# Casts ahead of transposes in the front of a batched product, and 14 small loads behind its last store

## The chip, the cores and the metric

The kernel runs on one core of one Trainium2 chip. The metric is device time in microseconds (us). The kernel before took 306.07 us, the median of three runs (305.9 to 306.18). A core has five engines that run side by side and meet only at semaphores: PE (TensorE, matrix products), DVE (VectorE), ACT (ScalarE), POOL (GpSimd) and SP (SyncE, which here only issues DMAs). Sixteen DMA engines move data between memory and the on-chip buffers.

## The reference

```python
batch, n_heads, seq_t, seq_s, channels = 8, 12, 512, 512, 64

def reference(x, y):
    return np.einsum('bhtc,bhsc->bhts', x, y).astype(np.float32)
```

There are 96 independent products of a 512x64 matrix with the transpose of another 512x64 matrix. Inputs and outputs are float32. The inputs are 25.17 MB in all and the output is 100.66 MB.

## The kernel before

**Tiling.** The 96 heads form six groups of 16. One group of x, or of y, is a contiguous block of 2 MB: 128 partitions of 64 rows with 64 channels each. So there are 12 loads; load 2g is x of group g, load 2g+1 is y of group g. A group has two halves, and half i (0 to 11, `NH` of them) gives two output tiles t = 2i and 2i+1. There are 24 tiles t; each is 128 partitions by 8192 float32 (4 MB) and is written by one store.

**Buffers.** Three large slots (`slot`, 4 MB each) serve as landing place of the loads and later as staging of the output tiles. A load takes half a slot (`place` 0 to 5), a store a whole one. Since the slots are shared, a load or an output tile can only enter where what was there has been read. `xk` keeps x of a group in bf16 and `yb` keeps y of half a group in bf16. `xb`, of which there is only one, holds x of one half rearranged for the transpose. `xT` and `yT` hold the transposed operands, two of each, one for even and one for odd halves.

**Steps.**
- `load(n, place)` (DMA issue on SP, L126) fetches a group.
- `keep_x(n)` (ACT, L114) casts 128x4096 x to bf16 in `xk`.
- `keep_y(n, half)` casts the 64 partitions of a half in two instructions, one for each half of the channels, on the engines that `in_front` names: DVE and POOL for half 0, DVE and ACT for half 1 (L116 for DVE and POOL, L114 for ACT).
- `mix(i, engine, parts)` copies x of half i from `xk` to `xb` in four parts of 32 partitions (L116).
- `turn_x(i)` and `turn_y(i)` are transposes on DVE (L184 and L197).
- `quarter(t, s, k, "act")` is eight matmuls into `pm` in PSUM (L212) and an eviction of 128x2048 from `pm` to a quarter of the slot on ACT (L114).
- `store(t, s)` (DMA issue on SP, L233) writes the slot to memory.

**Order.** Every engine runs its instructions in the order in which the code emits them; `emit` works out from what each reads and writes which semaphores it has to wait for (L82 where a wait stands alone). SP is such an engine too: if the next load waits for a cast, every later load and store stands behind it. A load into a half slot waits for the casts that read it (a y load for ACT, POOL and DVE). All loads and stores go through one DMA queue.

The front (from L238 to `store(2, 1)`) is written out by hand, with six loads issued at once and six more as half slots come free. Its part around the change, in the order before:

```python
        load(7, 3)
        mix(1, "pool", range(1, 4))
        turn_x(1)
        keep_x(4)
        load(8, 4)
        quarter(0, 0, 0, "act")
        keep_y(5, 0)
        keep_y(5, 1)
        load(9, 5)
        turn_y(1)
```

Behind the front a loop over t = 3 to 23 makes four quarters and a store for each tile, and prepares half i+2 on DVE after each odd t. At the end SP waits for the last store of each of the three slots.

Of the kernel before, what the change touches and what calls it, by code (L numbers as in the profile page):

```python
# [9 lines left out]
def kernel(  # L10
# [22 lines left out]
    nc = tc.nc  # L33
# [14 lines left out]
    fp32 = mybir.dt.float32  # L48
# [5 lines left out]
    xv = x.rearrange("b h t c -> (b h t c)").rearrange("(g p n) -> g p n", p=P, n=R * C)  # L54
# [5 lines left out]
    sb = ctx.enter_context(tc.tile_pool(name="sb", bufs=1))  # L60
# [2 lines left out]
    xks = [sb.tile([P, R, C], bf16, name=f"xk{i}") for i in range(NG - 1)]  # L63
    ybs = [sb.tile([P, R // 2 * D], u32, name=f"yb{i}") for i in range(2 * NG - 3)]
    xb = sb.tile([P, K * E * D], u32, name="xb")
    xTs = [sb.tile([P, K * D * E], u32, name=f"xT{i}") for i in range(2)]
    yTs = [sb.tile([P, D * R // 2], u32, name=f"yT{i}") for i in range(2)]
    pms = [ps.tile([P, 4, S], fp32, name=f"pm{i}") for i in range(2)]
    engines = {"act": nc.scalar, "dve": nc.vector, "pool": nc.gpsimd, "pe": nc.tensor, "sp": nc.sync}
    sems, ticks, known, snaps, writer, readers = {}, {}, {e: {} for e in engines}, {}, {}, {}  # L70

    def need(name, points):

        best = {}
        for p, v in points:
            if known[name].get(p, 0) < v:
                best[p] = max(best.get(p, 0), v)
        for p, v in list(best.items()):
            if any(snaps[q, w].get(p, 0) >= v for q, w in best.items() if q != p):
                del best[p]  # L80
        for p, v in best.items():
            engines[name].wait_ge(sems[p], v)  # L82
            known[name][p] = v
            for q, w in snaps[p, v].items():
                known[name][q] = max(known[name].get(q, 0), w)

    def emit(name, make, reads=(), writes=(), dma=None):

        points = [writer[r] for r in (*reads, *writes) if r in writer]
        points += [v for w in writes for v in readers.get(w, ())]  # L90
        if name == "pool" and name in ticks:
            points.append((name, ticks[name]))
        need(name, points)
        p, step = (name, 1) if dma is None else (f"dma{dma}", 16)
        if p not in sems:
            sems[p] = tc.alloc_semaphore(p)
        make().then_inc(sems[p], step)
        at = (p, ticks.get(p, 0) + step)
        ticks[p] = at[1]
        snaps[at] = {**known[name], p: at[1]}  # L100
        if dma is None:
            snaps[at][name] = at[1]
        for r in reads:
            readers.setdefault(r, []).append(at)
        for w in writes:
            writer[w], readers[w] = at, []
# [4 lines left out]
    def copy(name, dst, src, reads, writes):  # L111
        emit(
            name,
            lambda: nc.scalar.activation(dst, src, COPY)  # L114
            if name == "act"
            else engines[name].tensor_copy(dst, src),  # L116
            reads,
            writes,
        )

    def load(n, place):
        where[n] = place
        s, half = divmod(place, 2)
        emit(
            "sp",
            lambda: nc.sync.dma_start(  # L126
                slots[s][:, half * R * C:(half + 1) * R * C], (yv if n % 2 else xv)[n // 2]
            ),
            writes=[("slot", s, 2 * half), ("slot", s, 2 * half + 1)],
            dma=place,  # L130
        )

    def held(n):
        s, part = divmod(where[n], 2)
        return slots[s][:, part * R * C:(part + 1) * R * C], [("slot", s, 2 * part), ("slot", s, 2 * part + 1)]
# [6 lines left out]
    def home(g, half):  # L142

        if half == 0:
            return g % (NG - 1)
        return 1 if g == NG - 1 else NG - 1 + g % (NG - 2)

    def keep_y(n, half):
        src, reads = held(n)
        ys = src.rearrange("p (r c) -> p r c", c=C)  # L150
        b = home(n // 2, half)
        yv2 = ybs[b].bitcast(bf16).rearrange("p (j c w) -> p j w c", j=R // 2, w=2)
        for ch in range(2):
            copy(
                in_front[2 * half + ch],
                yv2[ch * 64:(ch + 1) * 64],
                ys[half * 64:(half + 1) * 64, :, ch * D:(ch + 1) * D].rearrange(
                    "p (j w) c -> p j w c", w=2
                ),
                reads,  # L160
                [("yb", b, ch)],
            )

    def mix(i, name, parts=range(4)):

        g, half = divmod(i, 2)
        xk = g % len(xks)
        xv2 = xb.bitcast(bf16).rearrange("p (k e c u) -> p k e c u", k=K, e=E, u=2)
        for part in parts:
            ch, u = divmod(part, 2)  # L170
            lo = half * 64 + u * D
            copy(
                name,
                xv2[part * D:(part + 1) * D, :, :, :, u],
                xks[xk][lo:lo + D, :, ch * D:(ch + 1) * D].rearrange("p (e k) c -> p k e c", k=K),
                [("xk", xk)],
                [("xb", part)],
            )

    def turn_x(i):  # L180
        half = i % 2
        emit(
            "dve",
            lambda: nc.vector.transpose(  # L184
                xTs[half].rearrange("p (k r e) -> p k e r", k=K, e=E),
                xb.rearrange("p (k e c) -> p k e c", k=K, e=E),
            ),
            [("xb", part) for part in range(4)],
            [("xT", half)],
        )  # L190

    def turn_y(i):
        g, half = divmod(i, 2)
        b = home(g, half)
        emit(
            "dve",
            lambda: nc.vector.transpose(  # L197
                yTs[half].rearrange("p (r j) -> p j r", r=D),
                ybs[b].rearrange("p (j c) -> p j c", c=D),
            ),  # L200
            [("yb", b, ch) for ch in range(2)],
            [("yT", half)],
        )
# [17 lines left out]
    def quarter(t, s, k, name):  # L221
        pm = filled[0] % 2
        filled[0] += 1
        half = t // 2 % 2
        ot = slots[s].rearrange("p (r s) -> p r s", s=S)
        emit("pe", lambda: products(t, k, pm), [("xT", half), ("yT", half)], [("pm", pm)])
        copy(name, ot[:, k:k + 4, :], pms[pm], [("pm", pm)], [("slot", s, k // 4)])
# [10 lines left out]
    with tc.tile_critical():  # L238
        for n in range(2 * BIG):
            load(n, n)  # L240
        emit(
            "dve",
            lambda: nc.vector.memset(xb, 0.0),  # L243
            writes=[("xb", part) for part in range(4)],
        )
        keep_x(0)
        mix(0, "dve")
        turn_x(0)
        keep_y(1, 0)
        keep_y(1, 1)  # L250
        turn_y(0)
        keep_x(2)
        load(6, 2)
        mix(1, "pool", range(1))
        keep_y(3, 0)
        keep_y(3, 1)
        load(7, 3)
        mix(1, "pool", range(1, 4))
        turn_x(1)
        keep_x(4)  # L260
        load(8, 4)
        quarter(0, 0, 0, "act")
        keep_y(5, 0)
        keep_y(5, 1)
        load(9, 5)
        turn_y(1)
        quarter(0, 0, 4, "act")
        keep_x(6)
        load(10, 2)
        quarter(0, 0, 8, "act")  # L270
        mix(2, "pool", range(1))
        keep_y(7, 0)
        keep_y(7, 1)
        load(11, 3)
        quarter(0, 0, 12, "act")
        store(0, 0)
        mix(2, "pool", range(1, 4))
        keep_x(8)
        quarter(1, 2, 0, "act")
        keep_y(9, 0)  # L280
        keep_y(9, 1)
        quarter(1, 2, 4, "act")
        keep_x(10)
        quarter(1, 2, 8, "act")
        quarter(1, 2, 12, "act")
        store(1, 2)
        keep_y(11, 0)
        turn_y(2)
        quarter(2, 1, 0, "act")
        quarter(2, 1, 4, "act")  # L290
        keep_y(11, 1)
        quarter(2, 1, 8, "act")
        quarter(2, 1, 12, "act")
        store(2, 1)
        turn_x(2)
        mix(3, "dve")
        for t in range(3, NT):
            s = (0, 2, 1)[t % 3]
            for k in range(0, K, 4):
                quarter(t, s, k, "act")  # L300
            store(t, s)
            i = t // 2 + 2
            if t % 2 and i < NH:
                turn_y(i)
                turn_x(i)
                if i + 1 < NH:
                    mix(i + 1, "dve")
        need("sp", [(f"dma{i}", ticks[f"dma{i}"]) for i in range(0, 2 * BIG, 2)])


# [28 lines left out]
```

## Time and profile before

| what | value |
|---|---|
| median of three runs | 306.07 us (305.9 to 306.18) |
| the profiled execution, device time | 305.63 us |
| its span in the profile | 303.8 us |
| busy: ACT | 213.1 us (70%) |
| busy: DVE | 154.0 us (51%) |
| busy: PE | 141.6 us (47%) |
| busy: POOL | 45.2 us (15%) |
| DMA moved | 125.95 MB, 415 GB/s over the span |
| DMA issue to landing, median | 21.8 us for a store, 14.1 for a load of x, 11.7 for a load of y |

All times in the profile count from the start of the span. A row of the timeline is: start, length, engine, line, operation, what is written and read, how many were merged, and in brackets the engine's idle time before it and what ended that. A row of the windows is: the stretch, its length, busy time and number of instructions of PE, PE's weight loads, DVE, ACT and POOL, then the granted PE clock, the busy share of the 16 DMA engines, and GB/s. An SPq row is SP's queue of DMA issues. The trace also records each DMA packet (start, length, size) and the time at which each of a DMA's 16 parts signalled its landing.

### The profile page before, as it was taken

The numbers are of one execution on the slowest core, as the hardware profiler recorded it, in microseconds if no ns is written. First come the engines' busy times: TensorE is split into PE (matmuls) and PEld (weight loads), VectorE is DVE, ScalarE is ACT, GpSimd is POOL, SyncE is SP. The second block draws the span as 40 slices with busy tenths as digits, with TensorE's granted clock in tenths as the row PEclk, the third lists the DMA queues.
The fourth block names the chain that finished last, engine by engine and source line by source line (L and its number), as shares of the span: only waits on it lengthen the run. The fifth ranks groups of instructions, "written<-read, shape, count | busy, mean of one in ns | idle before, by whom it ended". The sixth has DMA issues, their size and how long they took to land.

```text
span 303.8 us, 1880 instructions
## 1 busy us (share of the span) xinstructions
PE 141.6 (47%) x768; PEld 45.8 (15%) x768; DVE 154.0 (51%) x77; ACT 213.1 (70%) x109; POOL 45.2 (15%) x18
## 2 busy tenths in 40 slices
PE   0000543246655765457655665456456866474000
PEld 0000210011211211112111221112111221121000
DVE  2399679949695590944908529168094420000000
ACT  1656999689996797668866696668766786669000
POOL 0218979972000000000000000000000000000000
PEclk9999955558797878977677878977877667987555
DMA  7999996999999999999999999999999999999992
GB/s 272 427 436 425 423 427 227 431 414 438 427 423 444 436 429 423 441 428 431 429 444 423 427 440 436 425 427 444 431 427 429 440 431 423 444 429 427 431 444 125
DMA packets 5192, 125.95 MB, mean 415 GB/s; under 512 B 576, under 2 KB 576, under 8 KB 576
## 3 DMA queue, kind: packets, MB, share of 16 engines
q1 hardware_dynamic: 5184, 125.83, 97.1%
q8 instruction: 6, 0.10, 0.1%
q14 instruction: 2, 0.02, 0.0%
HBM read 25.17 MB, written 100.66 MB: 414 GB/s over the span
## 4 chain that ended last, share of the span: by engine, by line
DMA 51%; ACT 18%; POOL 12%; PE 5%; DVE 5%; issue 1%; ACTq 0%; POOLq 0%; SPq 0%
DMA out_dram<-slot 49%; ACT slot L114 15%; POOL xb L116 9%; PE pm L212 5%; POOL yb L116 3%; DVE xT L184 3%; DMA slot<-in_x_dram 3%; DVE xb L116 2%; ACT xk L114 1%; ACT yb L114 1%; ACTq L82 0%; POOLq L82 0%; SPq L334 0%; SPq L238 0%
## 5 line engine op out<-in xcount | busy, mean ns | idle before, releaser
L114 ACT ACTIVATE slot<-pm 128x2048 f32<-128x2048 f32 x96 | 175.4, 1876 | 49.9 <-DMA out_dram<-slot 44.1
L212 PE MATMUL pm<-yT,xT 128*64 128x512 bf16 x768 | 141.6, 516 | 137.5 <-ACT slot L114 106.7
L212 PEld LDWEIGHTS pm<-yT,xT 128*64 128x64 bf16 x768 | 45.8, 137 | 232.3 <-ACT slot L114 156.9
L116 DVE COPY xb<-xk 32x2048 bf16<-32x2048 bf16 x40 | 55.6, 1389 | 10.4 <-ACT xk L114 9.2
L197 DVE STREAM_TRANSPOSE yT<-yb 128x1024 uint32<-128x1024 uint32 x12 | 23.8, 1980 | 69.5 <-PE pm L212 69.4
L184 DVE STREAM_TRANSPOSE xT<-xb 128x2048 uint32<-128x2048 uint32 x12 | 46.0, 3836 | 4.9 <-POOL xb L116 4.9
L116 DVE CAST yb<-slot 64x2048 bf16<-64x2048 f32 x12 | 29.0, 2413 | 5.1 <-DMA slot<-in_y_dram 4.9
L114 ACT ACTIVATE xk<-slot 128x4096 bf16<-128x4096 f32 x6 | 21.7, 3617 | 12.0 <-DMA slot<-in_x_dram 12.0
L116 POOL COPY xb<-xk 32x2048 bf16<-32x2048 bf16 x8 | 26.3, 3284 | 9.6 <-DVE xT L184 9.2
L116 POOL CAST yb<-slot 64x2048 bf16<-64x2048 f32 x6 | 18.8, 3126 | 15.6 <-DMA slot<-in_y_dram 15.1
L114 ACT ACTIVATE yb<-slot 64x2048 bf16<-64x2048 f32 x6 | 14.8, 2474 | 5.0 <-DMA slot<-in_y_dram 4.9
L243 DVE MEMSET xb<- 128x2048 uint32 x1 | 1.8, 1765 | 1.4 <-SPq L238 1.4
L114 ACT ACT_TABLE_LOAD x1 | 1.3, 1283 | 0.9 <-SPq L238 0.9
L323 POOL MEMSET const-float32-0.0<- 128x1 f32 x1 | 0.1, 98 | 0.2 <-issue 0.2
L323 POOL MEMSET const-bfloat16-1.0<- 128x1 bf16 x1 | 0.1, 100 | 0.0
L323 POOL MEMSET const-float32-1.0<- 128x1 f32 x1 | 0.1, 98 | 0.0
L323 POOL MEMSET const-uint8-127<- 128x1 uint8 x1 | 0.1, 97 | 0.0
## 6 DMA issues: line engine op xcount, KB each, us to landing
out_dram<-slot SPq DMA_DIRECT2D x24, 4096.0 KB, 21.8
slot<-in_x_dram SPq DMA_DIRECT2D x6, 2048.0 KB, 14.1
slot<-in_y_dram SPq DMA_DIRECT2D x6, 2048.0 KB, 11.7
```

The lines of the kernel that those rows point to most:

```text
L114: lambda: nc.scalar.activation(dst, src, COPY)
L116: else engines[name].tensor_copy(dst, src),
L184: lambda: nc.vector.transpose(xTs[half].rearrange("p (k r e) -> p k e r", k=K, e=E), xb.rearrange("p (k e c) -> p k e c", k=K, e=E),),
L197: lambda: nc.vector.transpose(yTs[half].rearrange("p (r j) -> p j r", r=D), ybs[b].rearrange("p (j c) -> p j c", c=D),),
L212: last = nc.tensor.matmul(pms[pm][w * 64:(w + 1) * 64, j, :], xT[:, k + j, h, :], yT[:, h * S:(h + 1) * S], start=True, stop=True,)
L243: lambda: nc.vector.memset(xb, 0.0),
L323: nc = _bacc.Bacc("TRN2", target_bir_lowering=False, num_devices=1)
```

## The change

In the front:
- Part 3 of mix 1 goes from POOL to DVE. On DVE it stands behind the casts of load 3.
- `turn_x(1)`, which stood between the casts of loads 3 and 5 on DVE, goes behind the casts of load 5 (and behind the issue of load 9).
- `turn_y(1)`, which stood between the casts of loads 5 and 7, goes behind the casts of load 7 (and behind the issue of load 11).
- Mix 2 stays on POOL. Before, its part 0 stood ahead of the cast of load 7 and parts 1 to 3 ahead of the cast of load 9. Now parts 0 and 1 stand between the casts of loads 7 and 9, and parts 2 and 3 between those of loads 9 and 11.

At the end, behind the last store on SP, 14 loads of n = 2 to 15 rows of x with 16 float32 (64 bytes) each go into a new buffer `probe` that nothing reads. Each has a semaphore of its own and waits for nothing; SP waits for all of them behind the waits for the stores. In the changed file all lines behind the new buffer move down by one, and the 14 loads are L313.

```diff
+    probe = sb.tile([16, 256], fp32, name="probe")
...
         load(7, 3)
-        mix(1, "pool", range(1, 4))
-        turn_x(1)
+        mix(1, "pool", range(1, 3))
+        mix(1, "dve", range(3, 4))
         keep_x(4)
         load(8, 4)
         quarter(0, 0, 0, "act")
         keep_y(5, 0)
         keep_y(5, 1)
         load(9, 5)
-        turn_y(1)
+        turn_x(1)
         quarter(0, 0, 4, "act")
         keep_x(6)
         load(10, 2)
         quarter(0, 0, 8, "act")
-        mix(2, "pool", range(1))
         keep_y(7, 0)
         keep_y(7, 1)
         load(11, 3)
+        turn_y(1)
         quarter(0, 0, 12, "act")
         store(0, 0)
-        mix(2, "pool", range(1, 4))
+        mix(2, "pool", range(2))
         keep_x(8)
         quarter(1, 2, 0, "act")
         keep_y(9, 0)
         keep_y(9, 1)
+        mix(2, "pool", range(2, 4))
         quarter(1, 2, 4, "act")
...
+        for n in range(2, 16):
+            emit(
+                "sp",
+                lambda: nc.sync.dma_start(probe[:n, 16 * n:16 * n + 16], xv[0][:n, :16]),
+                writes=[("probe", n)],
+                dma=100 + n,
+            )
         need("sp", [(f"dma{i}", ticks[f"dma{i}"]) for i in range(0, 2 * BIG, 2)])
+        need("sp", [(f"dma{i}", ticks[f"dma{i}"]) for i in range(102, 116)])
```

## The prediction

> **What bounds the kernel now.** I read the page's slices first, then the queue's own waits, then the window where the slices dip, then the two engines that feed the wait, and the end of the span last.
>
> ```profile
> DMA  7999996999999999999999999999999999999992
> GB/s 272 427 436 425 423 427 227 431 414 438 427 423 444 436 429 423 441 428 431 429 444 423 427 440 436 425 427 444 431 427 429 440 431 423 444 429 427 431 444 125
> ```
>
> Each slice is 303.8/40 = 7.6 us. The 16 DMA engines are full from the second slice to the last but one, at about 430 GB/s, except in slice 7 (45.6 to 53.2 us), which moved 227 GB/s. So the span is 125.95 MB at the DMA rate, plus a start, plus a tail, plus that one hole. No compute engine sets the time except through this hole. The same stretch by the microsecond (the last two columns are the DMA share and GB/s):
>
> ```profile
> 46.00:47.00 1.00, 0.00 (x0) 0.00 (x0) 1.00 (x1) 0.98 (x2) 1.00 (x1) 0.50 0.84 360
> 47.00:48.00 1.00, 0.00 (x0) 0.00 (x0) 1.00 (x1) 1.00 (x1) 0.87 (x2) 0.50 0.01 0
> 48.00:49.00 1.00, 0.56 (x4) 0.31 (x6) 0.97 (x2) 0.98 (x2) 1.00 (x1) 0.50 0.00 0
> 49.00:50.00 1.00, 1.00 (x8) 0.24 (x4) 1.00 (x1) 1.00 (x1) 1.00 (x1) 0.50 0.93 180
> 50.00:51.00 1.00, 0.36 (x2) 0.00 (x0) 1.00 (x2) 1.00 (x1) 1.00 (x1) 0.50 0.65 147
> 51.00:52.00 1.00, 0.00 (x0) 0.00 (x0) 1.00 (x1) 1.00 (x1) 0.94 (x2) 0.50 0.75 311
> ```
>
> The queue is empty for two microseconds and then ramps up. SP's queue in order of time (start, length) shows why: after the load issued at 35.68 (number 8) nothing follows until 48.67 (number 9).
>
> ```profile
> 35.68 0.43 SPq L126 DMA_DIRECT2D slot<-in_x_dram  x1
> 48.67 0.33 SPq L126 DMA_DIRECT2D slot<-in_y_dram  x1
> 49.04 0.43 SPq L126 DMA_DIRECT2D slot<-in_x_dram  x1
> 55.72 0.33 SPq L126 DMA_DIRECT2D slot<-in_y_dram  x1
> ```
>
> Load 9 overwrites the half slot that holds y for group 2, so it waits for its casts. ACT's ended at 36.70 and POOL's at 42.73; the two on DVE were last, ending at 48.65:
>
> ```profile
> 40.15 3.88 DVE L184 STREAM_TRANSPOSE xT<-xb 128x2048 uint32<-128x2048 uint32 x1 [4.88 <-POOL xb L116]
> 43.88 4.77 DVE L116 CAST yb<-slot 64x2048 bf16<-64x2048 f32 x2
> 48.68 2.02 DVE L197 STREAM_TRANSPOSE yT<-yb 128x1024 uint32<-128x1024 uint32 x1
> 50.54 5.16 DVE L116 CAST yb<-slot 64x2048 bf16<-64x2048 f32 x2
> ```
>
> DVE stood idle for 4.88 us before the transpose, until POOL's last `xb` copy ended at 40.12, and the casts stood behind that transpose. POOL for the same time:
>
> ```profile
> 30.66 9.46 POOL L116 COPY xb<-xk 32x2048 bf16<-32x2048 bf16 x3
> 40.25 2.48 POOL L116 CAST yb<-slot 64x2048 bf16<-64x2048 f32 x1
> ```
>
> One more reading is needed to time the new order. A DVE copy or cast takes 1.3 us when POOL is idle. Every one that starts while POOL copies or casts takes until about 1.15 us after POOL's instruction ends (31.82 to 35.28 beside POOL's 30.66 to 34.12). POOL's own takes 2.48 us alone and 3.33 to 3.45 behind a DVE one. The two take turns; transposes stand outside this (POOL's 40.25 took 2.48 beside one).
>
> The end, by the microsecond:
>
> ```profile
> 298.00:299.00 1.00, 0.00 (x0) 0.00 (x0) 0.00 (x0) 0.00 (x0) 0.00 (x0) 0.50 0.53 229
> 299.00:300.00 1.00, 0.00 (x0) 0.00 (x0) 0.00 (x0) 0.00 (x0) 0.00 (x0) 0.50 0.08 33
> 300.00:301.00 1.00, 0.00 (x0) 0.00 (x0) 0.00 (x0) 0.00 (x0) 0.00 (x0) 0.50 0.08 33
> 301.00:302.00 1.00, 0.00 (x0) 0.00 (x0) 0.00 (x0) 0.00 (x0) 0.00 (x0) 0.50 0.00 0
> ```
>
> From 299.5 one DMA engine in 16 is at work (a share of 0.08). In the landing records 15 of the last store's 16 parts land by 300.38 and the last at 302.44: a straggler, 2.06 us late. The trace doesn't number the engines. From 302.44 to the end of the span are 1.38 us of closing barriers.
>
> **The change, part by part.**
>
> *1. Order on DVE and POOL, to load 9.* Up to 35.28 nothing differs. Then DVE takes over part 3 of mix 1 at once, where it stood idle: POOL copies until 37.58, so it ends at 37.58 + 1.15 = 38.73. POOL's cast of load 5 starts behind it, 37.64 + 3.4 = 41.05. DVE's first cast of load 5 takes its turn after that, 42.2, the second finds POOL waiting for load 7 (landed 43.04) and takes 1.3: 43.5. Load 9 is issued at about 43.55 instead of 48.67, load 10 right behind it (its `keep_x(6)` on ACT ended at 42.24). The engines run out of load 8 at 47, and 0.97 us lie between load 9's issue and its first packet (48.67 to 49.64), so anything issued by 46.0 leaves no hole. The margin is 2.45 us.
>
> *2. What the hole is worth.* Load 9 landed in full 8.44 us after load 8 (56.37 against 47.93); loads 0 to 8 landed 4.9 to 5.0 apart. So 3.5 us go. The low end is the time with nothing in flight, 47.5 to 49.6 = 2.1 us, should the slower ramp of load 9's packets and a slow load 11 be there anyway; I take 3.5, since the steady interval was measured on nine loads that had a load ahead of them, as load 9 will.
>
> *3. What is late next.* Turn_x(1) moves to 43.55 to 47.4. It is first read by the products of t=2, which started after 69 us, so this hides. Then DVE's two casts of load 7 alternate with POOL's part 0 of mix 2 (47.5 to 50.85) and end at 52.0; load 11 goes out at 52.05 instead of 55.72 and store 0 at 52.4 instead of 56.09 (its last eviction ends at 48.39, unchanged). Load 10's data ends at 56.7, so their margins are 3.6 and 8 us. Turn_y(1) now ends at 54.05 (before: 50.69), also first read by t=2; ACT's cast of load 9 waits for it (it writes the buffer that turn_y(1) reads), and is free itself only at 54.0. POOL takes y of load 9 between parts 1 and 2 of mix 2, at 54.4 to 57.8 instead of 61.61 to 65.05; DVE's casts end at 58.95. ACT then goes 54.1 cast, 56.5 eviction, 58.4 `keep_x(10)`, 62.0 and 63.9 evictions: store 1 at 65.85 instead of 68.89, needed by 69.7. Store 2 follows at 76.1 instead of 79.11, needed by 79.4. Mix 2 ends at 63.8 (before 61.48), but turn_x(2) stands behind casts of load 11 and starts at 68.5 (before 71.82). From store 3 on a slot is refilled about 7.5 us after its landing, with nearly 12 us of stores still ahead of it in the queue, so the whole stream moves up by what load 9 gained. Cost of all this: nothing, under the DMA queue; if a margin fails, its excess comes off the 3.5.
>
> *4. The 14 loads.* They stand behind store 23 on SP, which issues it at about 281.0 − 3.5 = 277.5. An issue of a load takes 0.33 to 0.69 us, so 14 take 5 to 10 us on SP, and the store lands 21.5 us after its own issue: hidden. Their data stand behind the store's in the same queue. They matter only where they follow the store on the straggler, or end after it. The price of one there: at least 0.02 us, from two markers of 9 ns each (the 4-byte packet that ends each part of a DMA); at most 0.33 us, the shortest instruction fetch of 8 KB, which is the nearest packet from memory shorter than a load's 16 KB (0.61). I take 0.05, near the low end, as a marker and 64 bytes are nearer to 4 bytes than to 8 KB. With 2 to 15 rows on so many engines each, about half of the 14 would lie on an unknown straggler: 7 x 0.05 = 0.35, rounded to 0.4 with a read's way to the end. The range is 0 (the straggler carries none, or they are done in its 2.06 us of lag) to 14 x 0.33 = 4.6. Nothing below nothing: the work is added behind a complete output.
>
> The Trainium skill, "DMA: Bandwidth & Descriptors", "Why a DMA increments its semaphore by 16 and not by 1", says that a load of n rows runs on the largest number up to 16 that divides both sides' slowest dimension, on the lowest-numbered engines; its "Latency and other measured facts" names engines 7 and 15 as usually the slow ones. By that the sum here would be 0 with 15 as the straggler and 8 small loads with 7; no record here numbers the engines. Against this change speaks its "Anatomy of one DMA", about 2 us fixed per DMA on the path it describes: 14 in series would be an estimated 28 us. But in this trace the stores land 9.7 us apart, which is their data at 433 GB/s with no gap, so what each has fixed is hidden by the next.
>
> *5. The closing waits.* SP waits on 17 semaphores instead of 3; two go into one instruction of 17 ns. In before the last store's is the last but one to be read, and in the changed program's listing too, so the others are passed earlier: 0, at most 7 x 0.07 = 0.5.
>
> **The sum.** Span 303.8 − 3.5 + 0.4 = 300.7. The profiled execution took 305.63, 1.83 more than its span: 302.5. It lies 0.44 under the median of 306.07, so against that: 306.07 − 3.1 = **303.0 us**.
>
> **The rivals.**
>
> *Slower: the small loads are not pipelined.* If each costs the straggler 0.33 us, like the 8 KB fetches, and all 14 are on it, the end is 306.07 − 3.5 + 4.6 = 307.2. It decides from 0.25 us per load (3.5/14) on. For it: one such packet never stood in this trace's queue, and 15 of 16 engines may carry them. Against: 32 KB packets took 1.213 and 16 KB ones 0.611, twice 0.611 less 0.009, so a packet's fixed part is near 9 ns when the queue is full. 7 in 100.
>
> *The hole stays.* If POOL takes both turns before DVE's casts, load 9 comes at 43.55 + 2 x 2.45 = 48.45 and gains 0.2: 306.2. One lost turn still fits the margin. For it: POOL's and DVE's requests fall within 0.1 us of one another at 37.6. Against: the turns alternated at every such place from 24 to 58 us. 5 in 100.
>
> *Half of it comes back later.* A new hole before load 11 or store 1 or 2, or a ramp that stays: 2.1 gained less 0.7 = 304.7. For it: store 1 and 2 have margins of only 3 to 4 us. Against: all they wait for moves up by 3 us too. 8 in 100.
>
> **How the numbers follow.** The forecast has 80 in 100, by itself 302.3 (nothing for the loads, and the 0.25 that runs differ by) to 303.9. With the case of half the gain the range is 302.1 to 304.9, which leaves out the other two. About 0.2% (0.6 us) can be told from no change: faster 0.88 (80 + 8), same 0.05 (the hole that stays), slower 0.07.
>
> **What would show it.** After: no slice under 400 GB/s in the front; load 9 issued near 43.5, load 11 near 52, store 0 near 52.4, store 1 near 66; a DVE copy of `xb` ending near 38.7 with the casts ahead of the transpose; 14 issues on SP near 278 to 285; the last store's last landing near 299 and the end 1.4 to 1.8 us after it. Wrong would be: SP stuck between the 14 issues, landings of them long after the straggler's, or DMA idle in a later slice.

## The result and the profile after

The changed kernel took 304.73 us (304.48 to 304.91), against 306.07 before: a ratio of 0.9957, 95% interval 0.9939 to 0.9975. That is 1.34 us faster. The forecast was 303.0, 3.1 us faster: the direction was right, the gain was far smaller.

The slices of the page after:

```profile
span 302.6 us, 1901 instructions
DMA  7999999999999999999999999999999999999990
GB/s 277 429 435 427 411 431 431 424 407 461 433 416 424 455 431 416 422 459 433 418 420 450 437 420 422 450 437 420 424 446 435 424 424 446 437 418 424 450 408 9
```

The dip of slice 7 is gone: no slice between the first and the last is under 407 GB/s. The last slice is new, with 9 GB/s: for its 7.6 us next to nothing moves. SP's queue after, in the stretch where loads 9 to 11 and store 0 are issued:

```profile
35.77 0.43 SPq L127 DMA_DIRECT2D slot<-in_x_dram  x1
43.74 0.33 SPq L127 DMA_DIRECT2D slot<-in_y_dram  x1
44.11 0.43 SPq L127 DMA_DIRECT2D slot<-in_x_dram  x1
52.31 0.33 SPq L127 DMA_DIRECT2D slot<-in_y_dram  x1
52.68 31.60 SPq L234 DMA_DIRECT2D out_dram<-slot  x4
```

Load 9 goes out at 43.74 (before: 48.67). The DMA engines stay busy (their share is the last column but one) where they were empty before:

```profile
47.00:48.00 1.00, 0.00 (x0) 0.00 (x0) 1.00 (x2) 1.00 (x1) 0.28 (x1) 0.50 1.13 475
48.00:49.00 1.00, 0.47 (x4) 0.22 (x6) 0.97 (x2) 0.98 (x2) 1.00 (x1) 0.50 0.96 410
```

DVE and POOL around it:

```profile
35.40 3.45 DVE L117 COPY xb<-xk 32x2048 bf16<-32x2048 bf16 x1
38.88 4.83 DVE L117 CAST yb<-slot 64x2048 bf16<-64x2048 f32 x2
43.74 3.92 DVE L185 STREAM_TRANSPOSE xT<-xb 128x2048 uint32<-128x2048 uint32 x1
...
30.69 6.99 POOL L117 COPY xb<-xk 32x2048 bf16<-32x2048 bf16 x2
37.81 3.37 POOL L117 CAST yb<-slot 64x2048 bf16<-64x2048 f32 x1
```

The casts of load 5 stand ahead of the transpose and end at 43.71.

The end is where the gain went. First the issues on SP, then the DMA engines by the microsecond, then SP's longest wait on the new loads (us in total, times, longest):

```profile
277.35 0.54 SPq L234 DMA_DIRECT2D out_dram<-slot  x1
277.93 16.32 SPq L313 DMA_DIRECT2D probe<-in_x_dram  x14
```
```profile
298.00:299.00 1.00, 0.00 (x0) 0.00 (x0) 0.00 (x0) 0.00 (x0) 0.00 (x0) 0.50 0.01 1
299.00:300.00 1.00, 0.00 (x0) 0.00 (x0) 0.00 (x0) 0.00 (x0) 0.00 (x0) 0.50 0.00 0
300.00:301.00 1.00, 0.00 (x0) 0.00 (x0) 0.00 (x0) 0.00 (x0) 0.00 (x0) 0.50 0.00 0
301.00:302.00 1.00, 0.00 (x0) 0.00 (x0) 0.00 (x0) 0.00 (x0) 0.00 (x0) 0.50 0.00 0
```
```profile
SPq L83 <- DMA probe<-in_x_dram: 5.6, 1, 5.6
```

All data have moved by 298.65, yet SP waits, and the span lasts until 302.6. The landing records tell for what. Each engine that carries a part of a DMA signals at the end of its part (a landing), and SP's wait ends with the last signal. The last landing of the last store and of each small load:

```
last store  299.04
2, 3, 4 rows   295.47  295.64  295.81
5 to 9 rows    299.23  299.42  299.61  299.80  299.99
10 to 15 rows  300.18  300.37  300.55  300.73  300.93  301.12
```

The loads of 2, 3 and 4 rows are done before the last store. From the load of 5 rows on, each has one part that lands behind the store's straggler, and each 0.19 us behind the one before it. The records don't number the engines. If a load of n rows uses the first n of them, as the prediction takes it, the straggler (the engine that ends last) is the fifth, and 11 signals of 0.19 stand behind its store. In the packet records the 11 loads lie at 298.51 to 298.65, 0.013 us for each with its marker: the bytes are through 2.5 us before the last signal.

The sum over the two profiles: the last store's landing moved from 302.44 to 299.04, −3.40; the landings behind it +2.08; from the last landing to the end 1.49 instead of 1.38, +0.11. That is −1.21, as the spans have it (303.82 to 302.61).

### The profile page after: what moved, and what is told of

Its sections match the earlier page's. It is cut to its first block, busy times and chain, and to the rows that moved or that the text cites. A ratio compares the mean times of both kernels' runs of the same rounds, so it can differ in the third digit from the quotient of the medians.

```text
span 302.6 us, 1901 instructions
## 1 busy us (share of the span) xinstructions
PE 145.5 (48%) x768; PEld 46.6 (15%) x768; DVE 156.1 (52%) x78; ACT 213.0 (70%) x109; POOL 42.2 (14%) x17
## 4 chain that ended last, share of the span: by engine, by line
DMA 51%; ACT 18%; DVE 14%; PE 6%; issue 2%; ACTq 0%; SPq 0%
DMA out_dram<-slot 49%; ACT slot L115 15%; DVE yb L117 8%; PE pm L213 6%; DVE xb L117 4%; DMA slot<-in_x_dram 3%; ACT xk L115 2%; DVE yT L198 1%; DVE xT L185 1%; ACT yb L115 1%; ACTq L83 0%; SPq L344 0%; SPq L239 0%
## 5 line engine op out<-in xcount | busy, mean ns | idle before, releaser
L213 PE MATMUL pm<-yT,xT 128*64 128x512 bf16 x768 | 145.5, 528 | 129.9 <-ACT slot L115 99.2
L213 PEld LDWEIGHTS pm<-yT,xT 128*64 128x64 bf16 x768 | 46.6, 139 | 227.9 <-ACT slot L115 150.3
L117 DVE COPY xb<-xk 32x2048 bf16<-32x2048 bf16 x41 | 58.8, 1433 | 10.5 <-ACT xk L115 9.2
L117 DVE CAST yb<-slot 64x2048 bf16<-64x2048 f32 x12 | 27.9, 2328 | 4.5 <-DMA slot<-in_y_dram 4.3
L117 POOL COPY xb<-xk 32x2048 bf16<-32x2048 bf16 x7 | 23.0, 3286 | 9.6 <-DVE xT L185 9.3
```

The source lines that it names most:

```text
L213: last = nc.tensor.matmul(pms[pm][w * 64:(w + 1) * 64, j, :], xT[:, k + j, h, :], yT[:, h * S:(h + 1) * S], start=True, stop=True,)
```

## The experiments

**The two parts, each alone.** The theory was now that the front gives 3.4 and the loads take 2.1 back, against a front worth only 1.3 with loads that cost nothing.

The changed kernel without the loads:

```diff
-        for n in range(2, 16):
-            emit("sp", ... dma=100 + n)
...
-        need("sp", [(f"dma{i}", ticks[f"dma{i}"]) for i in range(102, 116)])
```

> The new order of the front without the 14 loads. My theory (the front gives 3.4 us, and the loads cost 2.1 at the end, since each adds 0.19 us behind the last store on the engine that ends last): 302.6 us, last landing of the last store near 299.0, span near 300.5. Rival (the front is worth only 1.3 and the loads cost nothing): 304.7.

Measured: 302.05 us against 305.89 for the kernel before on the same chip, a ratio of 0.9873 (0.9858 to 0.9888). The theory held (302.6 expected) and the rival of 304.7 did not. In the profiles the last store landed at 298.96 and the span ended at 300.3, 3.5 less than before. SP now waits for stores alone:

```profile
SPq L82 <- DMA out_dram<-slot: 20.9, 1, 20.9
```

The kernel before with the 14 loads (the diff is the loop and the wait of the change, in `before`):

> The 14 loads behind the last store, with the front of before. My theory: 306.07 + 2.1 = 308.2, with 11 landings 0.19 us apart behind the last store's. Rival (the loads cost nothing by themselves): 306.1.

Measured: 308.34, a ratio of 1.0081 (1.0068 to 1.0095), as the theory had it. The last store landed at 303.11, and 11 signals behind it, the last at 305.19. The hole of slice 7 is there as before (229 GB/s), and so is the new empty slice at the end:

```profile
DMA  7999996999999999999999999999999999999990
GB/s 271 425 432 427 425 430 229 434 410 417 449 432 423 444 425 423 442 436 423 438 432 427 436 436 423 442 432 423 440 432 425 440 432 423 444 434 419 436 407 9
```

The two parts add up: −3.84 and +2.45 in the medians are −1.39, against −1.34 for both.

**What the loads' price goes by.** Fourteen loads of four rows, which should not reach the fifth engine, and fourteen of five rows, which should (the diff is that of four rows; with five, both 4s are 5):

```diff
-                lambda: nc.sync.dma_start(probe[:n, 16 * n:16 * n + 16], xv[0][:n, :16]),
+                lambda: nc.sync.dma_start(probe[:4, 16 * n:16 * n + 16], xv[0][:4, :16]),
```

> The changed kernel with 14 loads of 4 rows each instead of 2 to 15. They leave out nothing that the output needs. My theory (the straggler is the fifth engine, and four rows go to the first four): none on the straggler, so 302.6, as without loads, and within 0.3 of it. Rival (the price is one of 14 issues, semaphores and waits on SP): 304.7, as with the change.

> The changed kernel with 14 loads of 5 rows each. My theory: all 14 reach the fifth engine, 14 x 0.19 = 2.7 over the kernel without loads: 305.3, more than the changed kernel although there are 70 small rows instead of 119. Rival (the price goes by the number of rows): 2.1 x 70/119 = 1.2 over it, 303.9.

Measured: 302.36 with four rows (ratio 0.9889, 0.9876 to 0.9903) and 304.99 with five (0.9974, 0.9964 to 0.9984): both near the theory (302.6 and 305.3) and 1 us or more from the rivals (304.7 and 303.9). SP's waits tell them apart. With four rows it waits for the loads first and then still for the store (so in the running program the wait for the last store stands behind those for the loads, not ahead of them as in the code):

```profile
SPq L83 <- DMA probe<-in_x_dram: 3.1, 1, 3.1
SPq L83 <- DMA out_dram<-slot: 0.6, 1, 0.6
```

With five rows, only for the loads:

```profile
SPq L83 <- DMA probe<-in_x_dram: 6.2, 1, 6.2
```

The landings say the same. With four rows the last load lands at 298.55, ahead of the store's 298.98. With five the store lands at 298.93 and the loads from 299.12 to 301.57, 14 steps of 0.19. So neither 14 issues, 14 semaphores and 14 waits on SP, nor the number of rows, carries the price (70 rows end 2.64 us behind the store here, the change's 119 rows 2.08): it is the number of small loads that reach the engine that ends last, at 0.19 each. Four-row loads have the same spacing, 0.18, on the engines that they do use (the last landings of the 14 go from 296.20 to 298.55), but these engines end early. SP issues the four-row loads as slowly as the others and it costs nothing.

One load of 15 rows with 224 values each (the sum of the 14 in one DMA):

```diff
-        for n in range(2, 16):
+        for n in range(15, 16):
...
-                lambda: nc.sync.dma_start(probe[:n, 16 * n:16 * n + 16], xv[0][:n, :16]),
+                lambda: nc.sync.dma_start(probe[:n, :224], xv[0][:n, :224]),
```

> The changed kernel with a single load of 15 rows with 224 values each (14 times 64 bytes, in one DMA) instead of 14 loads. My theory (the price is one landing signal of 0.19 us per load on the straggler, not its bytes): 0.2 over the kernel without loads, 302.3 to 302.6. Rival (bytes or rows on the straggler): the same bytes and rows as in the changed kernel, 304.5.

Measured: 302.62 (0.989, 0.9876 to 0.9903). The store lands at 299.29 and the load at 299.48: one step of 0.19, as the theory had it. The other 0.4 or so over the front alone lies ahead of the store's landing; the two intervals overlap, so it isn't told from noise. In all these runs a load has one small packet and one signal on each engine, so no run prices the signal apart from the small packet ahead of it; that it is the signal is read from the packet records, 0.013 us against 0.19.

Rows of 256 bytes instead of 64 (the buffer `probe` is widened for them):

```diff
-                lambda: nc.sync.dma_start(probe[:n, 16 * n:16 * n + 16], xv[0][:n, :16]),
+                lambda: nc.sync.dma_start(probe[:5, 64 * (n - 2):64 * (n - 1)], xv[0][:5, :64]),
```

> 14 loads of 5 rows, each row 256 bytes instead of 64. My theory (per signal): as with 64 bytes, about 305.0, landings still 0.17 to 0.19 us apart. Rival (by bytes): four times 2.9 over the kernel without loads, above 310.

Measured: 305.11 (0.9975, 0.9965 to 0.9984) against 304.99 with 64 bytes, landings 0.18 to 0.19 apart. Going from 64 to 256 bytes doesn't matter.

**Does a signal cost the same in the middle of the stream?** The 14 loads ahead of the last store:

```diff
+            if t == NT - 1:
+                for n in range(2, 16):
+                    emit("sp", ... dma=100 + n)
             store(t, s)
```

> The 14 loads of the changed kernel stand ahead of the last store on SP instead of behind it. SP needs about 16 us for them, and the last store's issue moves from 277.4 to about 283.5, still ahead of the end of the store before it (287). My theory as it stands (what costs is the wait for a signal that nothing covers at the end; a small packet and its marker take 0.026 us of an engine): 11 x 0.026 = 0.3 over the kernel without loads, 302.4. Rival (each signal occupies the engine for 0.19 us wherever it stands): 2.1 over it, 304.3.

Measured: 304.02 (0.9936, 0.9924 to 0.9949). The median doesn't answer, because the run's premise failed. The loads kept SP until 284.93, the last store went out at 284.98, and that was late: some engines ran dry from about 285.0 on, not at 287, and at 285 to 286 the DMAs moved 202 GB/s. The straggler did not run dry, though, and its packets do answer. It ended the store before at 289.19, passed the 11 loads by 289.34, and started the last store's data at once; but the first two 32 KB packets of these took 1.97 and 1.81 us instead of 1.21. So 11 signals cost it 1.36 us, 0.12 each. I tried again with seven loads of five rows ahead of each of the last two stores, in time that SP has to spare, so that no engine runs dry:

```diff
+            if t in (NT - 2, NT - 1):
+                for n in range(2, 9) if t == NT - 2 else range(9, 16):
+                    emit("sp", ... probe[:5, ...] ...)
             store(t, s)
```

> 14 loads of 5 rows as in the run with five rows, but 7 of them ahead of each of the last two stores on SP. Seven take SP about 8 us, which it has idle between two stores, so neither store is issued late (the run with all 14 ahead of the last store delayed that one past the time at which the queue ran dry). Theory A (what costs is the chain of signals that nothing follows at the end): 14 x 0.026 = 0.4 over the front alone. Theory B (every signal holds its engine for 0.19 us wherever it stands): 2.7 over the front alone.

> The front without loads once more, beside the three others on one chip, as their measure: 302.0 to 302.3.

Measured on one chip: 303.76 (0.9932, 0.9919 to 0.9944) with the loads, 302.05 (0.9874, 0.986 to 0.9887) without. Both theories miss. The stores were issued in time (267.55 and 277.43). The straggler's landings of the last three stores came at 279.66, 289.98 and 300.24, instead of 279.44, 289.13 and 298.78 without loads. The 0.22 at the first of them lies ahead of all the loads' signals, so 14 signals cost the straggler 1.24 us, about 0.09 each: less than the 0.19 at the end, but seven times the 0.013 of a packet and its marker. The first four engines carry the same loads, but they end early: the 15th part of the last store landed at 296.67 with and 296.69 without.

The landings and packets of these two runs show what later data cover. In mid-stream the signals on the straggler come 0.19 to 0.20 us apart, as at the end: from the landing of the store before to the last signal 11 take 2.13 us, and twice 7 take 1.35 and 1.37. The data start at once, but one or two of the next packets last longer, by 1.36, 0.60 and 0.57 us in all. The difference is 0.77, 0.75 and 0.80: each time about 0.77 us of the signals is covered, and the rest is paid. What sets that 0.77 stays open.

**Which part of the front closes the hole.** Moving only `turn_x(1)` behind the casts of load 5, with part 3 of mix 1 left on POOL:

```diff
         mix(1, "pool", range(1, 4))
-        turn_x(1)
...
         load(9, 5)
+        turn_x(1)
         turn_y(1)
```

> The kernel before with one line moved: turn_x(1) behind the casts of load 5; no loads at the end, the copies of mix as before. By the turns of DVE and POOL: DVE's first cast of load 5 starts at 35.3 and ends at 38.7, the second at 42.2, POOL's copy of part 3 ends at 41.05 and its cast near 44.6, which now is the last: load 9 goes out near 44.7, ahead of 46.0, so the whole gain of the front, about 302.1. Rival (moving part 3 of mix 1 to DVE is needed for it): load 9 stays near 48 and 305.9.

Measured: 302.58 (0.9889, 0.9875 to 0.9902). Load 9 left at 44.79, as worked out; the time is 0.5 above the 302.1 expected:

```profile
44.79 0.33 SPq L126 DMA_DIRECT2D slot<-in_y_dram  x1
45.16 0.43 SPq L126 DMA_DIRECT2D slot<-in_x_dram  x1
53.70 0.33 SPq L126 DMA_DIRECT2D slot<-in_y_dram  x1
```

One line brings nearly all of the front's gain: on the same chip the whole front with one load of 15 rows behind it took 302.62. Moving only part 3 of mix 1 to DVE:

```diff
-        mix(1, "pool", range(1, 4))
+        mix(1, "pool", range(1, 3))
+        mix(1, "dve", range(3, 4))
         turn_x(1)
```

> The kernel before with part 3 of mix 1 on DVE, and no other move; no loads at the end. By the turns of DVE and POOL: DVE's copy ends at 38.85, turn_x(1) at 42.7, the casts of load 5 at 43.9 and, behind POOL's part 0 of mix 2, at 47.3. Load 9 goes out at 47.4 instead of 48.67, 1.3 earlier: 304.6. Rival (either part of the change closes the hole): 302.1. Rival (this part alone does nothing): 305.9.

Measured: 304.66 (0.9957, 0.9945 to 0.997). Load 9 left at 47.37, because its casts still stand behind the transpose, and the second takes its turn behind POOL's next copy:

```profile
47.37 0.33 SPq L126 DMA_DIRECT2D slot<-in_y_dram  x1
...
38.84 3.90 DVE L184 STREAM_TRANSPOSE xT<-xb 128x2048 uint32<-128x2048 uint32 x1
42.58 4.77 DVE L116 CAST yb<-slot 64x2048 bf16<-64x2048 f32 x2
```

Load 9's issue came 1.30 us earlier than in the kernel before, and the kernel 1.29 us. In this run, in which the queue still runs dry, the time follows load 9's issue one to one.

**Taking bytes off the straggler.** The front alone, with the last store in six pieces (one of 48 pairs of rows, one of three quarters of 16, four of the last quarters):

```diff
+        if t == NT - 1:
+            pieces = [(0, 48, 0, K * S), (48, 64, 0, 6144)] + [(p, p + 4, 6144, K * S) for p in range(48, 64, 4)]
+            for lo, hi, a, b in pieces:
+                emit("sp", lambda: nc.sync.dma_start(ov[i, z][lo:hi, :, a:b], slots[s][2 * lo:2 * hi, a:b]), ...)
+            return
```

> The front without loads, and the last store in six pieces: 48 of its 64 pairs of rows as before, then of the other 16 pairs three quarters of each row over 16 engines, and the last quarter in four pieces of 4 pairs, which go to the first four engines. This takes 16 KB (0.6 us) off the straggler and every engine from the fifth on, and puts 48 KB more on each of the first four, which end about 4 us before the straggler. My theory (the one straggling engine sets the end): 0.6 less one more signal of 0.19, so 0.4 below the front alone. Rival (the sum of bytes sets the end, and more pieces cost more): the same as the front alone or up to 1 above it.

Measured: 309.31 (1.0109, 1.0094 to 1.0124), 7.3 over the front alone, outside both expectations. The last slices fall to 341, 210 and 37 GB/s:

```profile
GB/s 273 428 430 433 415 437 426 411 428 454 426 413 456 422 420 457 419 422 456 415 426 452 422 430 441 418 443 439 418 437 435 422 452 422 420 456 418 341 210 37
```

The split made packets slow all over: of the 123 packets of 32 KB that started after 283 us, 34 took 1.4 to 5.0 us where a store's take 1.21, and the four pieces on the first engines ended last, at 306.21. All smaller pieces read the same 32 of the 128 partitions; that this slows them is a guess that no run here separates. As a test of whether fewer bytes on the straggler end the kernel earlier it says nothing.

The best of all these is the front alone, 302.05 us: 1.3% under the kernel before and 0.8% under the changed one.

## Why the prediction was right and wrong, point by point

*Step 1, the order up to load 9: right.* DVE's copy ended at 38.85 (38.73 worked out), POOL's cast at 41.18 (41.05), DVE's casts at 42.37 and 43.71 (42.2 and 43.5), and load 9 left at 43.74 (43.55). The rule of turns between DVE and POOL, read from 3.4 against 1.3 us, carried it, and the two one-part runs as well.

*Step 2, the hole: right.* The last store landed 3.40 us earlier; 3.5 was taken. Neither the low end of 2.1 nor a ramp that stays came about: load 9 landed 4.89 behind load 8 (before: 8.44), and load 10 again 4.89 behind load 9.

*Step 3, what is late next: right.* Load 11 left at 52.31 (52.05), store 0 at 52.68 (52.4), store 1 at 65.94 (65.85), store 2 at 76.14 (76.1). No margin failed.

*Step 4, the 14 loads: wrong in its size, and this is nearly the whole error.* That they cost only where they follow the store on the straggler was right. The term was 7 x 0.05, rounded to 0.4. It measured 11 x 0.19 = 2.08; of the 1.88 us by which the sum of the spans missed, 1.68 lie here. The count was out because the straggler turned out to be the fifth engine, which 11 of the 14 reach; 11 x 0.05 would still be only 0.55. The price was the larger fault: I costed a load by the time of its packet and marker (they do pass in 0.013 us, even less than the 0.02 of the low end), on the ground that 64 bytes are nearer to 4 bytes than to 8 KB, and not the signal that SP waits for. Before the change every DMA engine had several microseconds of data between two such signals, so their spacing was nowhere to be read. That the bounds of 0.02 and 0.33 held it is luck, since they too were the times of packets; they allowed no choice of 0.05 over, say, 0.2. (The shortest 8 KB fetch in the span is 0.31 us, not 0.33.) The issue on SP was out too: 0.79 to 1.28 us for each load, 16.3 in all instead of 5 to 10. It was hidden, as the run with four rows shows. In the expectations of the two runs in mid-stream the 0.026 us for a packet and its marker is twice what the packet records show.

On the Trainium skill's pages: "DMA: Bandwidth & Descriptors", "Why a DMA increments its semaphore by 16 and not by 1", is borne out, as a load of n rows shows n landings behind the data and one signal at the end of its issue. Engines 7 and 15, which "Latency and other measured facts" names as usually slow, were not it if the engines are counted as that page has it (its guess at a cause holds for DMAs issued from GpSimd, and all here are issued from SP); here it was the fifth. The 2 us of "Anatomy of one DMA", which are given for DMAs issued from GpSimd, did not add up in series: 0.19 did.

*Step 5, the closing waits: nearly right.* From the last landing to the end it took 0.11 us longer, where 0 was taken and at most 0.5 allowed. The loads' semaphores were not passed earlier: from 299.82 to 301.14 SP read them as they landed.

*The rivals and the range.* The slower one, loads that are not pipelined, had the right place and half the strength: it decides from 0.25 us per load on with all 14 on the straggler, and it came with 0.19 and 11. The hole did not stay, and nothing of it came back later. The forecast's own case ended at 303.9; the range reaches 304.9 only because of the case in which part of the hole comes back (304.7). That the measured 304.73 falls beside that number is luck: the time was lost at the end, not there.

## What to carry to other kernels

Where a DMA queue is the bound, look for the one dip in its slices, and price it by the landing interval there against the steady one; a cast that frees a load's buffer belongs ahead of a transpose that nobody awaits. Behind the last store a small DMA is not priced by its bytes: count its completion signals on the engine that ends last, here 0.19 us each, and put small transfers into one DMA or on engines that end early. With data behind them a few signals are covered, here about 0.77 us of them.

## What was not expected of the hardware

- One of the 16 DMA engines ended each kernel (but the one with the split store) 1.3 to 3.6 us behind the next slowest; where small loads tell, it was the fifth. Its lag grew: in the changed kernel its landings of stores lay 9.84 to 9.89 us apart in most of the second half, the earliest engine's 9.67 to 9.70.
- Completion signals on one engine land 0.17 to 0.20 us apart, though a packet and its marker pass in 0.013. In mid-stream 14 of them cost the straggler 1.24 us.
- A load of 5 rows with 64 bytes each takes SP 1.1 us to issue in most cases; the big stores took 0.54 and the big loads 0.33 to 0.69.
